# A hybrid decoder layer: both products of the rotary turn made by VectorE straight from PSUM

## Chip, cores, metric

One core of a Trainium2 chip. The metric is the device time of one execution in microseconds. The kernel before was timed three times; each comparison is against that kernel.

## What is computed

One layer with two groups of heads that run side by side, then a last RMSNorm. `x` is (1, 2048, 1024) in float32. The part that this document is about is the rotation of the attention heads' q and k by position:

```python
h = rmsnorm(x, norm_w) * (1.0 + scale) + shift
proj = h @ w_in                       # columns: deltanet q,k,v | z | b | a | at_q | at_k | at_v | at_z
o_dn = gated_delta_rule(...)          # 4 heads x 128: short convolution, chunked scan
aq, ak = rope(at_q, positions), rope(at_k, positions)   # 8 heads x 64
o_at = dilated_attention(aq, ak, av)
x = x + gate * (concat(o_dn * silu(z), o_at * silu(at_z)) @ w_out)
return rmsnorm(x)

def rope(x, positions):               # half = 32
    x1, x2 = x[..., :half], x[..., half:]
    return concatenate([x1 * cos - x2 * sin, x2 * cos + x1 * sin], axis=-1)
```

## The kernel before

Matrices are multiplied as three products of high and low halves (`three`, L612), so a 128x512 piece of the projection takes 24 matmuls, 8 blocks of depth by 3. The sequence is worked through in two halves of 1024 positions, each in two pieces `jj` of J = 512. The input projection is cut into 16 units of 256 columns; a unit is loaded, split into high and low halves (ScalarE casts `w_hi` at L580, POOL subtracts to `w_lo` at L581) and multiplied into PSUM tiles of the tag `ip`, of which there are two banks (`proj`, L622). Eight units are the deltanet heads' (`dn_unit`, L951: projection, convolution `cv_y`, then the solve `dn_intra` and `dn_solve` with `tmp_inv` and `rs_u`, and a scan `dn_scan` whose steps go between TensorE, VectorE and ScalarE by way of `y`, `state` and `o`). Units 8 to 11 are q and k of the attention heads and go through `rope_unit` (L1016). `ORDER` sets which units fill the time between two deltanet heads; each of the units 8 to 11 is done in both halves, so there are 16 pieces `jj` with two column tiles `ct` each: 32 rotations.

In `rope_unit` the columns are laid out so that `ct` 0 holds the first halves x1 of four heads and `ct` 1 their second halves x2. For each piece two tables (cosine and sine, 128x512) are loaded from DRAM (L1025). For each `ct` the projection ends in a PSUM bank; ScalarE copies the bank to SBUF (`rx`, L1031) and VectorE multiplies the bank by the cosine table (L1033; the trace calls all products `rp`). When both are there, POOL multiplies the copy of the other `ct` by the sine table (L1041, `rp` too), VectorE subtracts or adds (`rpc`, L1045), and a generator in the queue `late` splits the result (ScalarE `r_hi` L1052, POOL `r_lo` L1053) and writes it to DRAM (L1055), from where the attention reads it after the last rotation. The SBUF tiles of 128x512 come from one ring of nine buffers, tag `t512`, that the convolution, the gates and others share.

The program is written as generators that are stepped in turn (`tick`, L200): after each step of the main one, the solves, the scans and the rest each add a few instructions. The framework then lays out each engine's stream in a list by priority and by the times at which it estimates that instructions are ready; `Early` marks the scan's instructions as more urgent. An engine runs its stream in that order.

Of the kernel before, what the change touches and what calls it, by code (L numbers as in the profile page):

```python
# [11 lines left out]
F32 = mybir.dt.float32  # L12
# [3 lines left out]
OP = mybir.AluOpType  # L16
# [5 lines left out]
P = 128  # L22
KT = D // P
J = 512
# [6 lines left out]
T5 = 9  # L31
# [81 lines left out]
def kernel(ctx: ExitStack, tc: tile.TileContext, x, c_t, pos, w_mod, b_mod_t, b_gate,  # L113
# [3 lines left out]
    V, A, G = nc.vector, nc.scalar, nc.gpsimd  # L117
# [482 lines left out]
    def load_unit(u):  # L600
        w = w_tiles()
        if saved[u]:
            for a in range(2):
                dma(columns(u, w, a), wscr[u][a])
            return w
        for _ in unit_parts(u, w):
            pass
        saved[u] = True
        late.append(keep(u, w, KEEP))
        return w  # L610
# [11 lines left out]
    def proj(w, h, ct):  # L622

        ps = bank("ip")
        yield from three(ps, [lambda k, p=p: w[p][:, k, ct * P:ct * P + P] for p in range(2)],
                         [lambda k, p=p: h[p][:, k, :] for p in range(2)], KT)
        return ps
# [388 lines left out]
    def rope_unit(fa, u, js, hs, w):  # L1016
        w = w or load_unit(u)
        scr = (qscr, kscr)[u >= 10][u % 2]
        for jj in range(2):
            if jj:  # L1020
                yield "part"
            tab = [fa.tile([P, J], F32, name="tab", tag="t512", bufs=T5) for _ in range(2)]
            for i in range(2):
                c = ctab[i, js[jj]]
                dma(tab[i], bass.AP(tensor=c.tensor, offset=c.offset, ap=[[J, 32], [0, 4], [1, J]]))  # L1025
            xs, p1s = [], []
            for ct in range(2):
                ps = yield from proj(w, hs[jj], ct)
                by_class = ps.rearrange("p (i r) -> p r i", r=4)
                t = fa.tile([P, J], F32, name="rx", tag="t512", bufs=T5)  # L1030
                A.copy(t.rearrange("p (r i) -> p r i", r=4), by_class)  # L1031
                p1 = fa.tile([P, J], F32, name="rp1", tag="t512", bufs=T5)
                V.tensor_tensor(p1.rearrange("p (r i) -> p r i", r=4), by_class,  # L1033
                                tab[0].rearrange("p (r i) -> p r i", r=4), OP.mult)
                xs.append(t)
                p1s.append(p1)
                yield
            for ct in range(2):
                p1 = p1s[ct]
                p2 = fa.tile([P, J], F32, name="rp2", tag="t512", bufs=T5)  # L1040
                G.tensor_tensor(p2, xs[1 - ct], tab[1], OP.mult)  # L1041
                hi = fa.tile([P, J], F32R, name="r_hi", tag="r32", bufs=R3)
                lo = fa.tile([P, J], F32R, name="r_lo", tag="r32", bufs=R3)
                pc = fa.tile([P, J], F32, name="rpc", tag="t512", bufs=T5)
                V.tensor_tensor(pc, p1, p2, (OP.subtract, OP.add)[ct])  # L1045
                late.append(split(pc, hi, lo, scr, ct, js[jj]))
                if RY:
                    yield

    def split(pc, hi, lo, scr, ct, j):  # L1050
        yield from hop(RL)
        A.copy(hi, pc)  # L1052
        G.tensor_tensor(lo, pc, hi, OP.subtract)  # L1053
        for i, a in enumerate((hi, lo)):
            dma(scr[i, :, 32 * ct:32 * ct + 32, j].rearrange("h c t -> c h t"), a.bitcast(F32))  # L1055
# [5 lines left out]
    fa = fa_ctx.__enter__()  # L1061
# [346 lines left out]
    with (tc.tile_pool(name="start", bufs=1, side="left", reuse_waits="tile") as sp,  # L1408
          tc.tile_pool(name="fx0", bufs=2, side="left", reuse_waits="tile") as fx0):
        ordered[0] = OD  # L1410
        tab = tables(sp)
        h0, w12, wk, acc, xs = start(fa, sp, fx0)
# [337 lines left out]
```

## Time and profile before

| | us |
|---|---|
| median of three runs | 1560.82 (1558.38 to 1561.52) |
| profiled execution | 1564.69 |
| its span | 1562.9 |
| TensorE busy | 1433.8 |
| VectorE busy | 1066.2 |
| ScalarE busy | 656.0 |
| POOL busy | 466.1 |

The profile is one execution. Engines are named PE (TensorE; PEld is its loading of weights), DVE (VectorE), ACT (ScalarE), POOL and SP (which issues DMAs). An instruction is named by its line and by its tiles, out<-in. L138 stands for all that is recorded by the wrapper for urgent instructions, L149 for all matmuls. The idle time ahead of an instruction is put down to what ended last of what it waited for. A hole in PE is found in the timeline as the number in brackets.

### The profile page before, as it was taken

To read this page: it belongs to the slowest core of one execution; us is meant where nothing else is said; L and a number is where in the kernel's file an instruction comes from. 1 tells how busy PE (TensorE), PEld (TensorE's weight loads), DVE (VectorE), ACT (ScalarE), POOL (GpSimd) and SP (SyncE) were. 2 spreads that over 40 slices of the span, in tenths; PEclk is the share of its full clock that TensorE was granted. 3 is DMA by queue.
4 is the path that set the end of the run, shared out by engine and by line. 5 is a ranking of instruction groups with operands and counts; after the bars stand their busy time and mean duration, and the time that the engine had idled before them with its cause. 6 is when DMAs were issued, how large, how long until landed. Compare 5 with 4: busy or idle time off the path is not lost.

```text
span 1562.9 us, 28358 instructions
## 1 busy us (share of the span) xinstructions
PE 1433.8 (92%) x9848; PEld 1156.7 (74%) x9848; DVE 1066.2 (68%) x3305; ACT 656.0 (42%) x1864; POOL 466.1 (30%) x573
## 2 busy tenths in 40 slices
PE   3898999989879999998999999998899998999997
PEld 2687787767767787876777779886677776777776
DVE  6868745684786367587687766434476776889766
ACT  4435234335433753433243343222455554576444
POOL 2424253333452432041231320223121211142243
PEclk9999999999999999999999999999999999999999
DMA  8845562546573642454434515438877637363364
GB/s 245 277 135 192 162 206 81 176 133 212 178 225 97 226 132 87 155 177 129 152 99 129 159 39 154 148 106 259 248 224 212 205 108 229 89 197 104 105 226 162
DMA packets 256336, 257.08 MB, mean 164 GB/s; under 512 B 44993, under 2 KB 196673, under 8 KB 255681
## 3 DMA queue, kind: packets, MB, share of 16 engines
q1 hardware_dynamic: 253744, 246.88, 51.1%
q10 hardware_dynamic: 2448, 8.39, 1.4%
q8 instruction: 78, 1.28, 0.3%
q14 instruction: 66, 0.53, 0.1%
HBM read 164.31 MB, written 90.90 MB: 163 GB/s over the span
## 4 chain that ended last, share of the span: by engine, by line
PE 36%; DVE 10%; DMA 4%; ACT 2%; issue 2%; POOL 1%; SPq 1%; DVEq 0%; ACTq 0%; POOLq 0%
PE ip L149 16%; PE s L149 8%; PE tr L154 5%; PE po L149 4%; PE g L149 2%; PE sc L149 2%; DVE cv_y L693 1%; DMA sscr<-sta 1%; DMA wg<-in_w_mod_dram 1%; DVE tmp_inv L807 1%; DVE rs_u L282 1%; DVE pts L1251 1%; DMA y_lo<-in_w_out_dram 1%; DVE sm L1226 1%; DVE rs_u L281 0%
## 5 line engine op out<-in xcount | busy, mean ns | idle before, releaser
L149 PE MATMUL ip<-h_hi,w_hi 128*128 128x512 f32 x864 | 352.8, 410 | 6.0 <-ACT cv_r L688 4.7
L149 PE MATMUL ip<-h_hi,w_lo 128*128 128x512 f32 x864 | 352.6, 410 | 0.0
L149 PE MATMUL ip<-h_lo,w_hi 128*128 128x512 f32 x864 | 352.5, 410 | 0.0
L149 PEld LDWEIGHTS ip<-h_hi,w_hi 128*128 128x128 f32 x864 | 165.9, 192 | 39.3 <-ACT cv_r L688 5.6
L149 PEld LDWEIGHTS ip<-h_lo,w_hi 128*128 128x128 f32 x864 | 165.3, 191 | 32.2 <-issue 0.5
L149 PEld LDWEIGHTS ip<-h_hi,w_lo 128*128 128x128 f32 x864 | 165.1, 191 | 32.2 <-issue 0.8
L693 DVE SCALAR_TENSOR_TENSOR cv_y<-cv_r,cw,cv_y 128x512 f32<-128x512 f32 x144 | 116.0, 805 | 32.9 <-ACT cv_y L690 23.0
L581 POOL TENSOR_TENSOR w_lo<-w_raw,w_hi 128x512 fp32r<-128x512 f32 x72 | 97.0, 1357 | 112.4 <-ACT w_hi L580 84.7
L1226 DVE CUSTOM_DVE_ANT_0 sm<-s,mask 128x256 f32<-128x256 f32 (+3 forms) x256 | 107.9, 447 | 21.4 <-PE s L149 10.7
L154 PE MATMUL tr<-cst,p 128*128 128x128 f32 x568 | 95.3, 289 | 4.2 <-ACT p L1229 2.7
L1251 DVE COPY pts<-tr 128x512 f32<-128x512 f32 (+1 forms) x120 | 73.1, 616 | 30.7 <-PE tr L154 29.2
L1229 ACT ACTIVATE p<-sm,stb 128x128 f32<-128x128 f32 (+3 forms) x128 | 70.9, 555 | 52.4 <-DVE stb L1226 39.9
L1229 ACT ACTIVATE p<-sm,sta 128x256 f32<-128x256 f32 (+1 forms) x128 | 63.2, 495 | 68.7 <-DVE sta L1226 61.9
L154 PEld LDWEIGHTS tr<-cst,p 128*128 128x128 f32 x568 | 62.1, 142 | 25.4 <-issue 14.6
L695 ACT ACTIVATE cv_t<-cv_y 128x512 f32<-128x512 f32 x48 | 30.3, 631 | 117.6 <-DVE cv_y L693 114.1
L149 PE MATMUL ip<-w_hi,h_hi 128*128 128x264 f32 (+1 forms) x256 | 75.4, 295 | 2.0 <-DVE rp L1033 1.3
L149 PE MATMUL ip<-w_hi,h_lo 128*128 128x264 f32 (+1 forms) x256 | 75.0, 293 | 0.0
L149 PE MATMUL ip<-w_lo,h_hi 128*128 128x264 f32 (+1 forms) x256 | 74.9, 293 | 0.0
L807 DVE TENSOR_TENSOR tmp_inv<-xt_inv,blk 128x8 f32<-128x8 f32 (+14 forms) x240 | 65.6, 273 | 6.4
L580 ACT CAST w_hi<-w_raw 128x512 fp32r<-128x512 f32 x72 | 43.6, 617 | 49.4 <-DMA w_raw<-in_w_in_dram 40.9
L138 ACT ACTIVATE sqo<-o 128x128 f32<-128x128 f32 x64 | 19.8, 309 | 103.0 <-DVE o L138 97.3
L1041 POOL TENSOR_TENSOR rp<-rx,tab 128x512 f32<-128x512 f32 x32 | 41.5, 1312 | 57.5 <-ACT rx L1031 48.5
(470 smaller groups left out, 3372.9 us busy)
## 6 DMA issues: line engine op xcount, KB each, us to landing
w_raw<-in_w_in_dram SPq DMA_DIRECT2D x72, 256.0 KB, 3.9
ws<-w_hi SPq DMA_DIRECT2D x15, 1024.0 KB, 5.5
ws<-w_lo SPq DMA_DIRECT2D x15, 1024.0 KB, 7.4
w_hi<-ws SPq DMA_DIRECT2D x15, 1024.0 KB, 6.0
w_lo<-ws SPq DMA_DIRECT2D x15, 1024.0 KB, 7.5
xt<-in_x_dram SPq DMA_DIRECT2D x24, 512.0 KB, 5.2
wm<-in_w_mod_dram SPq DMA_DIRECT2D x32, 256.0 KB, 5.4
tab<-ctab SPq DMA_DIRECT2D x32, 256.0 KB, 3.3
```

Of the source, the lines that this page charges most:

```text
L138: return f(*a, **k)
L149: i = self.engine.matmul(ps, lhsT=lhsT, rhs=rhs, **k)
L154: i = self.engine.transpose(*a)
L580: A.copy(hi[:, s, 0:256], raw)
L581: G.tensor_tensor(lo[:, s, 0:256], raw, hi[:, s, 0:256], OP.subtract)
L693: V.scalar_tensor_tensor(y, r[:, n:n + J], cw[:, ti, n:n + 1], y, op0=OP.mult, op1=OP.add)
L695: A.activation(t, y, AF.Tanh)
L807: V.tensor_tensor(tmp[:, :, 0:i + 1], xt[:, :, 0:i + 1], b3[:, i:i + 1, 0:i + 1].to_broadcast([P, 4, i + 1]), OP.mult)
L1041: G.tensor_tensor(p2, xs[1 - ct], tab[1], OP.mult)
L1226: V.tensor_tensor_reduce(out=sm, in0=pp[hd], in1=masks, scale=-0.125, scalar=BIG, op0=OP.add, op1=OP.min, accum_out=st[:, slot, hd:hd + 1])
L1229: A.activation(pt, sm, AF.Exp, scale=-1.0, bias=st[:, slot, hd:hd + 1], accum_out=st[:, slot, 2 + hd:3 + hd])
L1251: V.tensor_copy(pts[:, 0:kn], pt[:, 0:kn])
```

## The change

ScalarE's copy and POOL's sine product are gone. In the loop over `ct`, VectorE multiplies the PSUM bank by the cosine table and then by the sine table, both in the transposed view `by_class`; the second loop only picks the two products that belong together. The rest of the rotation is the same.

```diff
-            xs, p1s = [], []
+            turned_ = []
             for ct in range(2):
                 ps = yield from proj(w, hs[jj], ct)
                 by_class = ps.rearrange("p (i r) -> p r i", r=4)
-                t = fa.tile([P, J], F32, name="rx", tag="t512", bufs=T5)
-                A.copy(t.rearrange("p (r i) -> p r i", r=4), by_class)
-                p1 = fa.tile([P, J], F32, name="rp1", tag="t512", bufs=T5)
-                V.tensor_tensor(p1.rearrange("p (r i) -> p r i", r=4), by_class,
-                                tab[0].rearrange("p (r i) -> p r i", r=4), OP.mult)
-                xs.append(t)
-                p1s.append(p1)
+                two = []
+                for i in range(2):
+                    t = fa.tile([P, J], F32, name=("rc", "rs")[i], tag="t512", bufs=T5)
+                    V.tensor_tensor(t.rearrange("p (r i) -> p r i", r=4), by_class,
+                                    tab[i].rearrange("p (r i) -> p r i", r=4), OP.mult)
+                    two.append(t)
+                turned_.append(two)
                 yield
             for ct in range(2):
-                p1 = p1s[ct]
-                p2 = fa.tile([P, J], F32, name="rp2", tag="t512", bufs=T5)
-                G.tensor_tensor(p2, xs[1 - ct], tab[1], OP.mult)
+                p1, p2 = turned_[ct][0], turned_[1 - ct][1]
```

## Rows read from the trace of the kernel before

**Rows 1.** The page, part 1: busy us (share of span) xinstructions.
```profile
PE 1433.8 (92%) x9848; PEld 1156.7 (74%) x9848; DVE 1066.2 (68%) x3305; ACT 656.0 (42%) x1864; POOL 466.1 (30%) x573
```
**Rows 2.** Busy time in the stretch of all rotations: length, busy per engine, clock, DMA.
```profile
150.00:1045.00 895.00, 845.36 (x5927) 683.94 (x5926) 589.73 (x1809) 331.97 (x968) 280.49 (x396) 0.98 0.47 148
```
**Rows 3.** Waits of PE from 150 to 1045 us: total us, times, longest.
```profile
PE sc L149 <- DVE state L138: 11.9, 12, 3.2
PE g L149 <- DVE qk L776: 10.0, 3, 6.6
...
PE ip L149 <- DVE rp L1033: 2.5, 3, 1.3
```
**Rows 4.** Groups by line and form, whole span: busy us, mean ns | idle before.
```profile
L1041 POOL TENSOR_TENSOR rp<-rx,tab 128x512 f32<-128x512 f32 x32 | 41.5, 1312 | 57.5 <-ACT rx L1031 48.5 <-issue 8.2 <-DMA oscr<-oc 0.5
...
L1045 DVE TENSOR_TENSOR rpc<-rp,rp 128x512 f32<-128x512 f32 x32 | 38.0, 1206 | 11.2 <-POOL rp L1041 11.2
...
L1033 DVE TENSOR_TENSOR rp<-ip,tab 128x512 f32<-128x512 f32 x32 | 22.0, 687 | 24.9 <-ACT rx L1031 24.8
...
L1031 ACT COPY rx<-ip 128x512 f32<-128x512 f32 x32 | 18.6, 581 | 30.4 <-PE ip L149 29.5 <-POOL xc L138 0.9
```
**Rows 5.** Instructions on the tile rp: ns min/median/max, first and last start.
```profile
L1033 DVE TENSOR_TENSOR rp<-ip,tab x32: 677/691/694, 169.0 to 1026.7; 128x512 f32<-128x512 f32 x32
...
L1045 DVE TENSOR_TENSOR rpc<-rp,rp x32: 678/926/1830, 179.3 to 1030.5; 128x512 f32<-128x512 f32 x32
```
**Rows 6.** Timeline of DVE near 430 us: start, length, instruction [idle before].
```profile
426.26 0.69 DVE L1033 TENSOR_TENSOR rp<-ip,tab 128x512 f32<-128x512 f32 x1
428.41 1.75 DVE L1045 TENSOR_TENSOR rpc<-rp,rp 128x512 f32<-128x512 f32 x1 [1.45 <-POOL rp L1041]
431.35 1.74 DVE L1045 TENSOR_TENSOR rpc<-rp,rp 128x512 f32<-128x512 f32 x1 [1.19 <-POOL rp L1041]
433.02 0.34 DVE L138 SCALAR_TENSOR_TENSOR y<-sc,sc,vs 128x128 f32<-128x128 f32 x1
...
433.42 0.17 DVE L807 TENSOR_TENSOR tmp_inv<-xt_inv,blk 128x8 f32<-128x8 f32 x1
```
**Rows 7.** Timelines of PE: the four holes that the sum names, and one matmul.
```profile
178.52 0.39 PE L149 MATMUL ip<-w_hi,h_hi 128*128 128x256 f32 x1 [1.26 <-DVE rp L1033]
...
402.55 0.47 PE L149 MATMUL ip<-h_hi,w_hi 128*128 128x512 f32 x1 [0.94 <-DVE rp L1033]
...
409.23 0.58 PE L149 MATMUL sc<-state,kq 128*128 128x128 f32 x1 [3.20 <-DVE state L138]
...
427.78 0.28 PE L149 MATMUL sc<-state,kq 128*128 128x128 f32 x1
...
434.07 0.38 PE L149 MATMUL sc<-y,inv 128*128 128x128 f32 x1 [2.29 <-ACT o L138]
```
**Rows 8.** Timeline of DVE near 405 us.
```profile
404.12 1.28 DVE L283 SCALAR_TENSOR_TENSOR xrs<-rs_u,xrs 128x8 f32<-128x8 f32 x1
405.44 1.20 DVE L281 TENSOR_TENSOR rs_u<-xrs 128x8 f32<-128x8 f32 x1
```
**Rows 9.** Timeline of POOL in the same stretch.
```profile
404.09 2.52 POOL L1041 TENSOR_TENSOR rp<-rx,tab 128x512 f32<-128x512 f32 x2
```
**Rows 10.** Busy time around two of the holes, columns as in Rows 2.
```profile
408.00:416.00 8.00, 6.77 (x23) 5.65 (x23) 7.29 (x23) 3.37 (x6) 3.67 (x3) 0.57 0.35 132
433.00:436.00 3.00, 1.93 (x9) 1.65 (x10) 2.73 (x11) 2.56 (x6) 1.40 (x2) 1.00 0.96 351
```
**Rows 11.** Timeline of DVE near 174 us.
```profile
173.72 0.98 DVE L807 TENSOR_TENSOR tmp_inv<-xt_inv,blk 128x8 f32<-128x8 f32 x1
...
174.94 1.01 DVE L807 TENSOR_TENSOR tmp_inv<-xt_inv,blk 128x12 f32<-128x12 f32 x1
```
**Rows 12.** Waits of SP's queue, whole span: the loads of the tables.
```profile
SPq L1025 <- POOL rp L1041: 11.7, 4, 8.6
```

## The prediction

> **What bounds the kernel now.** I read the page first: TensorE (PE) is busy 92% of the span, VectorE (DVE) 68% [rows 1]. So the time is TensorE's work plus the holes in it, and an edit on the other engines counts only where it opens, widens or closes a hole. Second, the stretch from 150 to 1045 us, where all 32 rotations lie (two pieces of 128x512 in each of 16 half stages; the cosine products start from 169.0 to 1026.7 us [rows 5]): TensorE is busy 845.36 of 895 us, so 49.6 us of holes are all that the change can act on directly [rows 2]. Third, what ends those holes: the rotation's own cosine product ends 2.5 us of them (it holds a projection's PSUM bank), the scan's state update on VectorE 11.9, the pair kk/qk on VectorE 10.0 [rows 3]. So VectorE's in-order queue is what TensorE waits for there, and the question is whether the change makes that queue shorter or longer at those places. Behind 1045 us no rotation runs, and the attention that reads the rotated q and k from DRAM starts later than that; a rotation that ends some us earlier or later moves nothing there.
>
> **What goes and what comes, engine by engine.** ScalarE loses 32 copies of 581 ns, 18.6 us; POOL loses 32 sine products of 1312 ns, 41.5 us [rows 4]. VectorE gets 32 sine products. They have the form of its cosine products (PSUM bank and one SBUF table in, SBUF out), which take 687 ns: 32 x 0.687 = +22.0 us [rows 4]. No DMA is added, moved or removed. Per half stage the ring of nine 128x512 buffers gives out 8 tiles in place of 10 (no copy, no separate sine tile: 2 tables, 4 products, 2 results), so a table's load on SP's queue, which four times waited for a POOL product to free a buffer, 11.7 us in all [rows 12], waits less; nothing behind it on SP's queue gets later. I count this at nothing, since TensorE's holes in [rows 3] are not ended by a DMA, and a gain is its only direction.
>
> **The port between VectorE and POOL.** The second thing VectorE loses is a stall. The combining subtraction or addition (two SBUF inputs) takes 678 ns at the least and 1830 at the most, the cosine product from PSUM 677 to 694 [rows 5]. The long ones lie beside a POOL product: in the two that start at 428.41 and 431.35 VectorE first idles 1.45 and 1.19 us for POOL's sine product, then needs 1.75 and 1.74 us [rows 6]; small instructions beside POOL's pair at 404.09 take 1.28 and 1.20 us where a small one elsewhere takes 0.17 [rows 6, 8, 9]. So a VectorE instruction with two SBUF inputs stands still until POOL's ends; one with a PSUM input does not. [...] With POOL's products gone the 32 combinations, 38.0 us at a mean of 1206 ns [rows 4], fall to somewhere between 690 ns (22 us in all) and no gain at all, since POOL still makes the low halves of weights and of the rotated tiles; I take 850 ns, nearer the free value because the partner that stood directly beside them is what goes: 38.0 - 27.2 = -10.8. The 11.2 us for which VectorE waited for POOL's product [rows 4] go whole. The cosine product waited 24.8 us for ScalarE's copy [rows 4], since both read one bank and the trace shows them one after the other; VectorE will now wait for TensorE's last matmul itself, so each such wait shrinks by up to one copy of 0.58. How many there are the row doesn't say, so between 0 and -18.6 (all 32); I count a fifth, -3.7, the value near no gain, since a busy VectorE comes to most of them late anyway. VectorE's time, busy and blocked together: +22.0 - 10.8 - 11.2 - 3.7 = -3.7 us, bounds +22.0 - 0 - 11.2 - 0 = +10.8 and 22.0 - 16 - 11.2 - 18.6 = -23.8. In total, then, VectorE's queue hardly changes; it is the places that decide.
>
> [...]
>
> **The holes, one by one** [rows 7].
> - At 434.07, 2.29 us: the scan's y (VectorE) started at 433.02 only because the two combinations ahead of it waited for POOL and were slowed by it [rows 6]. Without POOL's products they would follow the cosine product of 426.26 and the new sine product, 426.26 + 0.69 + 0.69 + 2 x 0.69, and end by 429 to 430; the matmul that y reads had begun at 427.78 [rows 6, 7]. The hole goes: -2.3.
> - At 409.23, 3.20 us, for the state update. Ahead of it on VectorE two small instructions lost 1.28 - 0.17 and 1.20 - 0.17 = 2.14 us to POOL's pair [rows 8, 9]; two sine products of 0.69 come in ahead of it. Net -0.76, the hole about 2.4. [...] Estimate from the row: 6.77 us busy x (1 - 0.57) = 2.9 us lost to the clock. A hole of 2.4 us is nearer to the 2.29 that kept the clock than to the 3.20 that lost it, so I count the 2.9 as saved, with 0 as the other bound: -3.7 together.
> - At 178.52, 1.26 us, for the bank: the cosine product stood behind two small instructions of 0.98 and 1.01 us beside POOL's pair, the first of them 0.17 elsewhere [rows 6, 11]: -1.65. The bank now comes free one product later: +0.69. Net -0.96.
> - At 402.55, 0.94 us, for the bank, where VectorE was merely late: +0.69.
> - Elsewhere a state update may stand behind an added product. Of the other 11 waits for it [rows 3] between none and all do; I take about half, five. There 0.69 comes and the stretch of a combination (1.206 - 0.69 = 0.5) goes: +0.2 each, +1.0.
> Sum: -2.3 - 3.7 - 1.0 + 0.7 + 1.0 = -5.3 us. The profiled execution took 1564.69 us (span 1562.9 and 1.8 around it), so 1559.4 by its own time; it ran 3.9 us above the median of 1560.82, and I give the forecast against that median: **1555.5 us**.
>
> **Rivals.**
> - *Hidden anyway.* Holes are closed and others open a little later, as TensorE meets the next late instruction; or the clock falls all the same behind 409. The sum without the clock is -2.4, and with nothing kept 0: 1558.5 to 1561. For it: the directly ended holes are 2.5 us only [rows 3]. Against: TensorE is 92% busy, so what it gains it mostly keeps.
> - *VectorE becomes late (slower).* Each added product delays what is queued behind it by 0.69 us, two per half stage. Where it lies ahead of a state update, a y or a kk/qk for which TensorE already stands, and no POOL stall is lifted in the same place, the hole widens by it. It decides from the point where more of TensorE's holes have such a product ahead of them than have a POOL stall. Price: eight such places (somewhat under half of the 18 waits counted in [rows 3]) x 0.69 = +5.5, 1566.3 us; if one of them grows past 3 us, the clock adds 2.9 as above. For it: those 18 waits are all VectorE's. Against: its busy and blocked time falls by my count.
> - *The planner lays the streams differently.* The order on each engine is set at the build from priorities and estimated ready times. With other costs on three engines it can put an instruction ahead of or behind a scan step anywhere behind 168 us, in the attention too. The price is one large hole more or less: the longest that ends with VectorE's qk is 6.6 us [rows 3], so 1554 or 1567, either sign.
> - *It doesn't do what it says:* the same products with the same tables, so no.
>
> **How the numbers follow.** About 0.2% (3.1 us) is what a measurement of this kernel can tell from no change. The forecast has 0.58, of which 0.44 lands beyond 0.2% and 0.14 inside (its clock part fails); hidden 0.12, all inside; VectorE late 0.16, slower; the planner 0.14: 0.06 faster, 0.02 the same, 0.06 slower. Faster 0.50, same 0.28, slower 0.22. The forecast's own range is 1550 (all holes named gone whole, 2.29 + 3.20 + 2.9 + 1.26 + 0.94 = 10.6) to 1560. The range is 1550 to 1567: its lower end is that one, its upper end takes in late VectorE and the bad side of the planner, and what is left out is several such mishaps at once.
>
> **What the profile after would show.** Right: sine and cosine products both at about 690 ns, 64 of them, 44 us; combinations near 850 ns with no wait for POOL; POOL about 41 and ScalarE about 19 us less busy; TensorE busy as before; no hole of 2.3 us behind a rotation, and the clock full where it fell at 409. Wrong: combinations still near 1200 ns (then other POOL work was the partner), holes on the state update or on the bank longer than 11.9 and 2.5 us in all, or large holes in places with no rotation near, which would be the planner's.

## Result and profile after

The changed kernel takes 1545.63 us in the median of six runs (1538.31 to 1550.44), the kernel before 1562.59 in six (1558.38 to 1563.82). The ratio is 0.9884, 95% interval 0.9863 to 0.9905: some 18 us less, where 5.3 were forecast and the range ended at 1550.

The profiled execution took 1541.81 us, its span is 1540.0. Against the span before, 1562.9, that is -22.9, more than the 18 of the ratio: 1541.81 lies low among the six of after, and the 1564.69 of the profiled execution before above its six. The page of after, part 1, in the columns of [rows 1]:

```profile
PE 1425.7 (93%) x9848; PEld 1153.4 (75%) x9848; DVE 1064.3 (69%) x3337; ACT 641.0 (42%) x1832; POOL 421.0 (27%) x541
```

TensorE does the same 9848 instructions. Its holes, span less busy time, went from 1562.9 - 1433.8 = 129.1 to 1540.0 - 1425.7 = 114.3, that is -14.8; the other -8.1 is busy time, the same work at a higher clock (granted share from 150 to 1045 us 0.98 [rows 2], in after 0.99). VectorE has 32 instructions more, 21.8 us of them, and is not busier: 1066.2 [rows 1] to 1064.3.

The groups of the rotation in after, columns as in [rows 4]:

```profile
L1051 POOL TENSOR_TENSOR r_lo<-rpc,r_hi 128x512 fp32r<-128x512 f32 x32 | 42.8, 1339 | 108.1 <-ACT r_hi L1050 43.8 <-issue 31.2 <-PE g L149 15.5
...
L1043 DVE TENSOR_TENSOR rpc<-rc,rs 128x512 f32<-128x512 f32 x32 | 26.5, 852 | 0.4
...
L1033 DVE TENSOR_TENSOR rc<-ip,tab 128x512 f32<-128x512 f32 x32 | 21.9, 685 | 15.6 <-PE ip L149 10.7 <-DMA tab<-ctab 3.4 <-POOL xc L138 1.4
L1033 DVE TENSOR_TENSOR rs<-ip,tab 128x512 f32<-128x512 f32 x32 | 21.8, 681 | 1.3 <-ACT xsq L529 1.2
```

The new sine product `rs` costs what the cosine product costs, the combination fell from 1206 [rows 4] to 852 ns, and its wait for POOL is gone. Those are the sizes that the forecast gave them.

TensorE's waits, first of after, then the rows of before that [rows 3] left out; both from 150 to 1000 us, where the holes of before sum to 49.6 us and those of after to 35.5 (neither has one from there to 1045):

```profile
PE sc L149 <- DVE state L138: 9.8, 9, 2.3
PE g L149 <- DVE qk L776: 8.3, 3, 5.3
PE g L149 <- DVE xt_inv L809: 4.9, 2, 2.8
PE g L149 <- issue: 3.7, 2, 2.7
...
PE g L149 <- ACT w L138: 1.9, 2, 1.5
PE ip L149 <- DVE rs L1033: 1.3, 1, 1.3
...
PE sc L149 <- ACT y L138: 0.3, 1, 0.3
```
```profile
PE g L149 <- issue: 9.0, 2, 4.8
PE sc L149 <- ACT o L138: 4.4, 4, 2.3
PE g L149 <- DVE xt_inv L809: 3.9, 3, 1.6
...
PE sc L149 <- ACT y L138: 2.2, 3, 1.1
```

The steps of the scan (`state`, `o`, `y`) ended 11.9 + 4.4 + 2.2 = 18.5 us of holes before and 9.8 + 0.3 = 10.1 after: there lies more than half of what the holes lost. The product that holds a projection's bank ended 2.5 us before and 1.3 after, but that isn't a gain: one of the three holes, 0.94 us at 402.55, is 1.09 in after and only stands under another name (`xrs`).

**Where along the way.** The order of TensorE's matmuls is nearly the same in both kernels, so they can be matched one to one. The lead of after (start before less start after) grows like this, steps under 0.45 us left out and neighbouring ones taken together:

| matmul, start before / after | lead | what it is |
|---|---|---|
| 178.52 / 177.67 | +1.4 | named in the forecast |
| 199.08 / 199.12 | -1.3 | new: the bank waits for the added sine product |
| 206.27 / 205.44, 276.90 / 276.41, 283.62 / 282.19 | +0.8, -1.0, +0.9 | a bank, a longer wait for `state`, one for `y` gone |
| 327.88 / 322.25, and the matmuls behind it | +3.2, +2.4 | hole put down to "issue", clock behind it |
| 335.52 / 329.05 to 368.76 / 365.92 | -5.2 | given back: two longer holes, a fall of the clock behind the second, small steps |
| 395.61 / 390.82 | +2.0 | mostly order: nine small matmuls that stood ahead of it come later in after; a hole of 0.30 is gone |
| to 402.55 / 398.72 | -1.0 | seven of the nine; the named hole, 0.94, is 1.09 |
| 409.23 / 402.38, and behind it | +3.0, +2.8 | named: hole, clock |
| 416.95 / 407.73 to 419.61 / 411.73 | -1.8 | the other two of the nine, new wait for `state` |
| 434.07 / 423.82 | +2.5 | named |
| 448.77 / 437.43 to 478.91 / 465.88 | +2.8 | +4.2 as at 328, of which 1.4 are given back |
| 478.91 / 465.88 to 828.70 / 806.77 | +8.9 | twelve steps of 0.5 to 1.8, two of them back; six in the scan |

The named places give 1.4 - 0.2 (the hole at 402.55 alone) + 5.8 + 2.5 = 9.5; the forecast had 6.3 for them. The other 13 us of the 22.9 came in places for which it had a loss of 1.0. One of them, before: VectorE, then POOL, then TensorE (start, length, instruction).

```profile
791.36 1.28 DVE L281 TENSOR_TENSOR rs_u<-sc 128x4 f32<-128x4 f32 x1
792.68 0.96 DVE L282 SCALAR_TENSOR_TENSOR rs_u<-rs_u,ss 128x4 f32<-128x4 f32 x1
793.68 0.96 DVE L283 SCALAR_TENSOR_TENSOR sc<-rs_u,sc 128x4 f32<-128x4 f32 x1
794.56 0.34 DVE L138 SCALAR_TENSOR_TENSOR y<-sc,sc,vs 128x128 f32<-128x128 f32 x1
```
```profile
791.35 1.28 POOL L1053 TENSOR_TENSOR r_lo<-rpc,r_hi 128x512 fp32r<-128x512 f32 x1
792.59 1.04 POOL L716 TENSOR_TENSOR gmghi<-cst,ghi 128x512 fp32r<-128x512 f32 x1
793.59 1.03 POOL L716 TENSOR_TENSOR gmglo<-cst,glo 128x512 fp32r<-128x512 f32 x1
```
```profile
795.36 0.49 PE L149 MATMUL sc<-y,inv 128*128 128x128 f32 x2 [1.74 <-ACT o L138]
```

Three small instructions of a solve, which take 0.16 to 0.17 us elsewhere, end each with one of POOL's. The scan's `y` stands behind them on VectorE, and TensorE waits for it. No rotation product is there; POOL's three are reads that after still makes. The same matmul in after starts at 774.01 without a hole; there VectorE's `y` came before POOL's next long read (VectorE, then POOL):

```profile
771.84 0.34 DVE L138 SCALAR_TENSOR_TENSOR y<-sc,sc,vs 128x128 f32<-128x128 f32 x1
```
```profile
772.72 1.74 POOL L1051 TENSOR_TENSOR r_lo<-rpc,r_hi 128x512 fp32r<-128x512 f32 x1 [0.90 <-DMA qscr<-r_hi]
```

### The profile page after: what moved, and what is told of

Same layout as the page of the kernel before. It is cut to its first block, busy times and chain, and to the rows that moved or that the text cites. A ratio compares the mean times of both kernels' runs of the same rounds, so it can differ in the third digit from the quotient of the medians.

```text
span 1540.0 us, 28271 instructions
## 1 busy us (share of the span) xinstructions
PE 1425.7 (93%) x9848; PEld 1153.4 (75%) x9848; DVE 1064.3 (69%) x3337; ACT 641.0 (42%) x1832; POOL 421.0 (27%) x541
## 3 DMA queue, kind: packets, MB, share of 16 engines
q8 instruction: 78, 1.28, 0.3%
## 4 chain that ended last, share of the span: by engine, by line
PE 44%; DVE 12%; DMA 7%; ACT 3%; issue 2%; POOL 1%; SPq 1%; DVEq 0%; ACTq 0%; POOLq 0%
PE ip L149 21%; PE s L149 8%; PE tr L154 6%; PE po L149 4%; PE g L149 3%; PE sc L149 3%; DVE cv_y L693 1%; DMA xt<-in_x_dram 1%; DVE tmp_inv L807 1%; DMA yscr<-m_x 1%; DMA wg<-in_w_mod_dram 1%; DMA sscr<-sta 1%; DVE rs_u L282 1%; ACT hf L557 1%; DVE rs_u L281 1%
## 5 line engine op out<-in xcount | busy, mean ns | idle before, releaser
L581 POOL TENSOR_TENSOR w_lo<-w_raw,w_hi 128x512 fp32r<-128x512 f32 x72 | 96.0, 1343 | 120.0 <-ACT w_hi L580 94.2
L1227 ACT ACTIVATE p<-sm,stb 128x128 f32<-128x128 f32 (+3 forms) x128 | 70.9, 555 | 49.6 <-DVE stb L1224 38.0
L1051 POOL TENSOR_TENSOR r_lo<-rpc,r_hi 128x512 fp32r<-128x512 f32 x32 | 42.8, 1339 | 108.1 <-ACT r_hi L1050 43.8
L807 DVE TENSOR_TENSOR tmp_inv<-xt_inv,blk 128x8 f32<-128x8 f32 (+14 forms) x240 | 61.1, 254 | 6.0
```

What stands on the lines that cost most here:

```text
L581: G.tensor_tensor(lo[:, s, 0:256], raw, hi[:, s, 0:256], OP.subtract)
L807: V.tensor_tensor(tmp[:, :, 0:i + 1], xt[:, :, 0:i + 1], b3[:, i:i + 1, 0:i + 1].to_broadcast([P, 4, i + 1]), OP.mult)
L1227: A.activation(pt, sm, AF.Exp, scale=-1.0, bias=st[:, slot, hd:hd + 1], accum_out=st[:, slot, 2 + hd:3 + hd])
```

## The experiments

Two theories. *The port:* while POOL reads SBUF with a sine product, VectorE's instructions with two SBUF inputs stand still, and that alone cost the 18 us. *The wait:* the combination waited for POOL's product and the cosine product for ScalarE's copy, and lifting these waits gave the gain. "Port" is a name only: no run shows by what way POOL's reading stops VectorE. Beside them stand the extra work on VectorE (rival "VectorE becomes late") and the order of the streams (rival "the planner").

**Both back, as work that nobody reads.** The changed kernel, with ScalarE's copy and POOL's product on top; the combination doesn't depend on them.

```diff
+                rx = fa.tile([P, J], F32, name="rx", tag="t512", bufs=T5)
+                A.copy(rx.rearrange("p (r i) -> p r i", r=4), by_class)
+                xs.append(rx)
...
+                idle = fa.tile([P, J], F32, name="rp2", tag="t512", bufs=T5)
+                G.tensor_tensor(idle, xs[1 - ct], tab[1], OP.mult)
```

> The changed kernel, with ScalarE's copy and POOL's sine product put back beside it: they run at their old place and cost, but nothing reads POOL's product, so it is work on top that leaves the output as it is. Theory of the wait (what was gained is that VectorE's queue no longer stands at the combination until ScalarE and POOL have passed the half on): the gain stays for the most part, 10 to 17 us under the kernel before, combinations wait for POOL 0 us. Theory of the port (what was gained is that POOL's 41.5 us no longer block VectorE's two-SBUF-input instructions): the gain goes, 0 to +5 us against the kernel before, since VectorE also does 22 us more; combinations back to 1.1 to 1.2 us. Theory of the planner: any value, with no relation to holes behind rotations.

Measured: 1565.16 against 1565.13, ratio 1.0004 (0.9981 to 1.0026). The whole gain is gone although no result of POOL's is used. The groups:

```profile
L1044 POOL TENSOR_TENSOR rp<-rx,tab 128x512 f32<-128x512 f32 x32 | 46.1, 1441 | 59.6 <-ACT rx L1031 19.5 <-DVE rc L1036 12.8 <-issue 12.7
...
L1048 DVE TENSOR_TENSOR rpc<-rc,rs 128x512 f32<-128x512 f32 x32 | 31.1, 985 | 6.8 <-POOL rp L1044 4.3 <-issue 2.1
```

The combination is slower than in after (985 against 852 ns), though not back at the 1.1 to 1.2 us expected. It still waits 4.3 us for POOL, where the kernel before has 11.2 [rows 4]; as it uses no result of POOL's, this can only be for a buffer of the ring. So the wait for the result is not the cause, and what is left of the wait is too short for 18 us; in the run with POOL copies below, 8.5 us of it go with a time 12 us shorter. It may still be POOL's reading, its time, or the copy.

**Only the copy back.** The first three added lines of the diff above.

> The changed kernel with ScalarE's copy put back, read by nobody. Theories of the wait and of the port alike: within 3 us of the changed kernel, 14 to 20 us under the kernel before, as the copy only holds the PSUM bank along with VectorE's first product. If the 18.6 us of ScalarE are the cause: the gain goes, 0 to -5.

Measured: 1547.17, ratio 0.9902 (0.9876 to 0.9928). The gain stays within the interval of after; the copy, and the cosine product's wait for it (19.4 us, against 24.8 [rows 4]), cost some 3 us by the two ratios, which can't be told from zero.

**VectorE's work alone.** The kernel before, with 32 sine products on VectorE that nobody reads.

```diff
+                idle = fa.tile([P, J], F32, name="rs", tag="t512", bufs=T5)
+                V.tensor_tensor(idle.rearrange("p (r i) -> p r i", r=4), by_class,
+                                tab[1].rearrange("p (r i) -> p r i", r=4), OP.mult)
```

> The kernel before with the 32 sine products on VectorE from PSUM on top, read by nobody; POOL and ScalarE do all they did. It measures the price of 22 us of VectorE alone, which the prediction put at 0.7 to 5.5 us: +1 to +6 us against the kernel before. If VectorE is where TensorE's holes come from, as much as +15; if its time is free there, 0 +- 2.

Measured: 1564.01, ratio 1.0006 (0.9986 to 1.0027): 22 us more on VectorE, from PSUM, cost nothing.

**POOL as long, but writing only.** As in the first experiment, the product replaced by three fills of about its length.

```diff
-                G.tensor_tensor(idle, xs[1 - ct], tab[1], OP.mult)
+                G.memset(xs[1 - ct], 0.0)
+                G.memset(idle, 0.0)
+                G.memset(idle[:, 0:192], 0.0)
```

> As the run with both put back, but in the place of POOL's sine product stand three fills with zeros (512, 512 and 192 columns), which wait for the same copy and together take about as long, 1.3 us; they write SBUF and read nothing. Work on top; the output stays. Port theory (POOL's product costs because it reads SBUF through what VectorE's second input needs): the time stays that of the copy alone put back, 12 to 17 us under the kernel before. Theory of POOL's queue (it costs because weights' low halves and the scan's small copies stand behind it on POOL): the gain is gone as in the run with both put back, 0 +- 3 us. In the trace, small VectorE instructions beside a fill are at 0.17 us under the port theory in either case; what decides is the time.

Measured: 1548.86 against 1566.08, ratio 0.9902 (0.9866 to 0.9937). The page's part 1, then the groups:

```profile
PE 1428.9 (92%) x9848; PEld 1154.7 (75%) x9848; DVE 1067.5 (69%) x3337; ACT 658.6 (43%) x1864; POOL 462.2 (30%) x637
```
```profile
L1045 POOL MEMSET rp<- 128x512 f32 x32 | 16.9, 527 | 3.2 <-DVE rs L1036 2.5 <-DVE rc L1036 0.7
L1044 POOL MEMSET rx<- 128x512 f32 x32 | 16.8, 526 | 74.3 <-ACT rx L1031 71.0 <-issue 3.3
...
L1046 POOL MEMSET rp<- 128x192 f32 x32 | 8.2, 259 | 1.6
```

POOL is as busy as before (462.2 against 466.1 [rows 1]), in the same place of its queue and behind the same copy, and the gain is there. Between this run and the first lie 1.0 point of ratio, some 16 us. TensorE's matmuls have the same order in both. They differ in whether POOL reads; besides, the product holds the sine table's buffer, which the fills don't, but TensorE's waits in the first run have a DMA in them for 0.3 us only. So it is the reading. It shows in single instructions too. The same small instruction with two SBUF inputs takes 1.24 us in the first run beside the product (VectorE, POOL) and 0.15 in this one beside a fill:

```profile
398.67 1.24 DVE L912 SCALAR_TENSOR_TENSOR so<-so,eq 128x4 f32<-128x4 f32 x1
```
```profile
398.60 1.29 POOL L1044 TENSOR_TENSOR rp<-rx,tab 128x512 f32<-128x512 f32 x1
```
```profile
395.54 0.15 DVE L912 SCALAR_TENSOR_TENSOR so<-so,eq 128x4 f32<-128x4 f32 x1
```
```profile
395.29 0.53 POOL L1045 MEMSET rp<- 128x512 f32 x1
```

**Short fills.** Two fills of 8 columns in the product's place: the waiting at the head of POOL's queue without the time.

> The same with two fills of 8 columns each: POOL only stands and waits for ScalarE's copy at that place, and works some 0.1 to 0.2 us. If the waiting at the head of POOL's queue is the cost: the gain is gone or half gone, 0 to -8 us against the kernel before. Under the port theory, and if it is POOL's time: 12 to 17 us under the kernel before, like the copy alone.

Measured: 1543.97, ratio 0.9862 (0.9831 to 0.9894), more under the kernel before (some 21 us) than the 12 to 17 expected, but not to be told from the long fills or from after.

**POOL reading one input.** The product replaced by two copies of the same tile.

```diff
-                G.tensor_tensor(idle, xs[1 - ct], tab[1], OP.mult)
+                G.tensor_copy(idle, xs[1 - ct])
+                G.tensor_copy(idle, xs[1 - ct])
```

> As the run with both put back, with two POOL copies of 512 columns (one SBUF input each, some 0.55 us) in the place of the sine product; work on top. It asks whether POOL must have two inputs to block VectorE. If any reading blocks: the gain goes by as much as the copies are long, to 0 to -6 us against the kernel before; if only two-input instructions block: 14 to 18 us under the kernel before, as with the fills.

Measured: 1553.43 against 1564.54, ratio 0.9930 (0.9908 to 0.9951).

```profile
L1049 DVE TENSOR_TENSOR rpc<-rc,rs 128x512 f32<-128x512 f32 x32 | 28.4, 899 | 8.8 <-POOL rp L1045 7.0 <-POOL rp L1044 1.5
L1044 POOL COPY rp<-rx 128x512 f32<-128x512 f32 x32 | 24.2, 756 | 60.5 <-ACT rx L1031 19.7 <-DVE rs L1036 13.3 <-DVE rc L1036 11.6
...
L1045 POOL COPY rp<-rx 128x512 f32<-128x512 f32 x32 | 23.7, 739 | 1.8
```

Against the copy alone (0.9902), 47.9 us of one-input reading cost some 4 us, which the intervals don't tell from nothing; against after (0.9884) some 7. The 46.1 us of two-input reading cost 16 and 19. So one-input reading costs less than two-input reading, between the two forecasts. Whether that is because each block is half as long (739 to 756 against 1441 ns) or because POOL reads one operand in place of two isn't settled.

**The sine product on VectorE, from the copy.** The kernel before, with L1041 moved from POOL to VectorE and nothing else (`G.tensor_tensor` becomes `V.tensor_tensor`).

> The kernel before with one letter changed: VectorE in place of POOL makes the sine product from ScalarE's copy in SBUF; the copy stays. TensorE's order is nearly that of the kernel before. Theory of the wait: POOL's part of the passing-on is gone and ScalarE's is left, so a half to all of the gain: -8 to -17 us. Theory of the port: POOL's products are gone, so the whole gain, -15 to -19, less up to 3 because the new products themselves have two SBUF inputs and can stand still beside POOL (mean over 0.8 us in place of 0.69). If ScalarE's copies are the cause: 0 to -3 us.

Measured: 1552.17, ratio 0.9922 (0.9893 to 0.9951). Two thirds of the gain come from that alone:

```profile
L1045 DVE TENSOR_TENSOR rpc<-rp,rp 128x512 f32<-128x512 f32 x32 | 29.7, 930 | 0.6
L1041 DVE TENSOR_TENSOR rp<-rx,tab 128x512 f32<-128x512 f32 x32 | 23.7, 742 | 0.5 <-issue 0.5
```

From SBUF the product has two SBUF inputs and takes 742 ns in the mean, with POOL's other reads still there (`r_lo` 44.9 us, `w_lo` 97.1); from PSUM, in after, it takes 681. Two operations follow the matmul here, and copying its output to SBUF ahead of the second brought nothing: 0.9922 with the copy, 0.9884 without.

**The two products in the other order.** The changed kernel with sine before cosine: the same work, a handful of instructions elsewhere in the streams.

```diff
-                for i in range(2):
+                for i in (1, 0):
```

> The changed kernel with the two products of a bank in the other order, sine ahead of cosine: the same work and waits, but the planner lays some instructions in other places. It measures what such a shift alone does: theory of the planner, 5 us or more either way from the changed kernel; otherwise within 3 us of it, 15 to 20 under the kernel before.

Measured: 1540.22 against 1564.54, ratio 0.9842 (0.9825 to 0.9858), some 6 us better than after (2 to 11 by the two intervals). A shift of order without any work in it is thus worth some 6 us; so much of any difference here, the 18 us too, can be order. The whole isn't: the five kernels without POOL's product or a reading in its place (after, the copy alone, both fills, this one) lie 15 to 25 us under the kernel before, and the two that keep the product (both back, VectorE's work alone) within 1 us of it.

**More of POOL's reading taken away.** If reading is the price, POOL's other two-input work has one too. The changed kernel with the subtraction `r_lo` (32), with every second `w_lo` (36 of 72), with both, and with `r_lo` and all `w_lo` on VectorE:

```diff
-        G.tensor_tensor(lo, pc, hi, OP.subtract)
+        V.tensor_tensor(lo, pc, hi, OP.subtract)
```

> The changed kernel, and the rotated tiles' low halves (32 subtractions with two SBUF inputs) also on VectorE in place of POOL. POOL loses 42.8 us of reading, VectorE gains some 27 us. Port theory: POOL's other readings cost as its products did, so faster than the changed kernel, 5 to 15 us, 22 to 30 under the kernel before. Theory that only the rotation's own wait mattered: no gain, 0 to +5 against the changed kernel.

Measured: 1535.15 against 1566.08, ratio 0.9810 (0.9768 to 0.9852).

```diff
-            G.tensor_tensor(lo[:, s, 0:256], raw, hi[:, s, 0:256], OP.subtract)
+            (G, V)[g % 2].tensor_tensor(lo[:, s, 0:256], raw, hi[:, s, 0:256], OP.subtract)
```

> The changed kernel, and every other low half of the weights (36 of 72) on VectorE in place of POOL: POOL loses 48 us of reading, VectorE gains 30 us. Port theory: faster than the changed kernel by 3 to 10 us. If VectorE is full by now: slower by up to 10.

Measured: 1540.00, ratio 0.9833 (0.9807 to 0.9858).

> Both moves that made the changed kernel faster, together: the rotated tiles' low halves and half of the weights' on VectorE. Port theory with time left on VectorE: 32 to 40 us under the kernel before. If VectorE has become the bound by then (60 us of subtractions more than in the changed kernel): no better than the first move alone, 26 to 31 under.

Measured: 1522.02 against 1564.54, ratio 0.9729 (0.9706 to 0.9752).

```diff
-            G.tensor_tensor(lo[:, s, 0:256], raw, hi[:, s, 0:256], OP.subtract)
+            V.tensor_tensor(lo[:, s, 0:256], raw, hi[:, s, 0:256], OP.subtract)
...
-        G.tensor_tensor(lo, pc, hi, OP.subtract)
+        V.tensor_tensor(lo, pc, hi, OP.subtract)
```

> The same with all of the weights' low halves on VectorE: POOL loses some 140 us of reading against the changed kernel, VectorE gains some 85. Port theory alone: 38 to 50 us under the kernel before. VectorE as the bound: slower than the run with half of them.

Measured: 1499.06, ratio 0.9579 (0.9549 to 0.9609), the best of all: 66 us less than before, 47 less than after. Its page, part 1, some groups, and the stretch from 150 to 1000 us:

```profile
PE 1416.2 (95%) x9848; PEld 1149.0 (77%) x9848; DVE 1057.4 (71%) x3441; ACT 643.4 (43%) x1832; POOL 292.8 (20%) x437
```
```profile
L581 DVE TENSOR_TENSOR w_lo<-w_raw,w_hi 128x512 fp32r<-128x512 f32 x72 | 49.4, 695 | 31.5 <-ACT w_hi L580 31.1
...
L1051 DVE TENSOR_TENSOR r_lo<-rpc,r_hi 128x512 fp32r<-128x512 f32 x32 | 22.6, 705 | 3.0 <-DMA qscr<-r_hi 1.7 <-DMA kscr<-r_hi 0.6 <-ACT o L138 0.5
...
L1043 DVE TENSOR_TENSOR rpc<-rc,rs 128x512 f32<-128x512 f32 x32 | 21.3, 683 | 2.3 <-issue 2.2
```
```profile
150.00:1000.00 850.00, 832.11 (x5939) 679.76 (x5938) 583.54 (x1894) 314.38 (x914) 137.43 (x282) 1.00 0.48 155
```

VectorE takes on 49.4 + 22.6 = 72.0 us and its busy time falls from 1064.3 to 1057.4: 79 us of its other instructions' busy time had been standing still. The combination is at its free value, 683 ns. TensorE's holes in the stretch are 850 - 832.11 = 17.9 us, against 35.5 in after in the same stretch of time, and the clock is 1.00. Taking both away gains more than either, and all of it most; the first two runs can't be told apart by their intervals. The last gained more than the 38 to 50 us that the port theory gave it, and the four don't separate the port from a second effect: VectorE makes a `w_lo` in 695 ns where POOL took 1343, so weights may be ready earlier.

## Why the prediction was wrong

The sign was right, the size was not: -5.3 forecast, -18 measured, below the range. Step by step:

- *What goes and what comes.* VectorE +22.0: measured +21.8. POOL -41.5 and ScalarE -18.6: POOL's busy time fell by 45.1, ScalarE's by 15.0. Right.
- *The port.* Combinations 850 ns, measured 852, which is luck in part: 850 was a choice between 690 and 1206, and the kernels without the product show 798 to 865. The wait for POOL's product -11.2, measured -10.8 (11.2 to 0.4). Right. The cosine product's waits -3.7: its idle time went from 24.9 to 15.6, and the sine product has 1.3, so -8.0. Too small, but the copy's run shows that this is worth little.
- *"VectorE's queue hardly changes."* This is the first wrong sentence. The ledger took up stalls of the combinations alone. Busy time: +21.8 for the sine products and 26.5 - 38.0 = -11.5 for the combinations make +10.2 with the cosine products' -0.1; measured 1064.3 - 1066.2 = -1.9. So 12.1 us were saved in other VectorE instructions that stood beside POOL's products. With the waits it is -1.9 - 10.8 - 8.0 = -20.7 against the forecast's -3.7, next to its lower bound of -23.8.
- *The holes, one by one.* 434.07: -2.5 for -2.3, right. 178.52: -1.4 for -0.96, right there, but 20 us on the bank waits 1.27 us for an added product, and the gain is gone. 409.23: -3.0 for -0.76, and the clock -2.8 for -2.9; the hole was mis-sized. 402.55: from 0.94 to 1.09, +0.15 for +0.69, and by another route: in after VectorE first stands 1.55 us for the load of a table, which the forecast counted at nothing. Of these, in after (PE, then VectorE):

```profile
199.12 0.36 PE L149 MATMUL ip<-w_hi,h_hi 128*128 128x256 f32 x1 [1.27 <-DVE rs L1033]
...
398.72 0.47 PE L149 MATMUL ip<-h_hi,w_hi 128*128 128x512 f32 x1 [1.09 <-DVE xrs L533]
...
402.38 0.71 PE L149 MATMUL sc<-state,kq 128*128 128x128 f32 x4 [0.20 <-DVE state L138]
...
411.73 0.71 PE L149 MATMUL sc<-state,kq 128*128 128x128 f32 x4 [1.14 <-DVE state L138]
```
```profile
397.20 0.69 DVE L1033 TENSOR_TENSOR rc<-ip,tab 128x512 f32<-128x512 f32 x1 [1.55 <-DMA tab<-ctab]
```

  The 3.20 us hole is 0.20. Ahead of `state` the two stalls beside POOL's pair [rows 8, 9] are gone, as forecast, and the combination that stood there before has moved behind it. A wait of 1.14 us for the next `state` is new.
- *"Elsewhere ... +1.0".* This is the step that failed. It looked at the holes that have a rotation product directly ahead of them, took five more waits for `state` at +0.2 each and every other place at nothing. In these places the lead grew by 13 us in the profiled pair. That POOL's reading is the cause of the sum is shown by the runs with products and with fills. How it reaches a single place was only followed in the example at 795 us: remaining reads of POOL's (`r_lo`, `gmghi`, `gmglo`) fall beside a solve before and behind it in after. That taking the products out of POOL's queue is what shifted them there is argued, not shown. Such a hole is put down to `state`, `o`, `y` or "issue", and as the example shows it needs no rotation near it.
- *The clock.* The forecast took one drop, at 409, and worked out its 2.9 us from the first row of [rows 10]. That a hole of 2.4 us would keep the clock was its estimate, which no run shows: in after this hole is 0.20 us, and the clock from 401 to 409 is 1.00. There were others: 0.62 and 0.66 before in stretches of which the matched ones in after have 1.00 and 0.83 (columns as in [rows 2], first two of before, then two of after):

```profile
325.00:334.00 9.00, 6.12 (x46) 4.92 (x47) 8.66 (x20) 1.93 (x4) 0.77 (x3) 0.62 0.43 126
462.00:472.00 10.00, 6.29 (x50) 5.07 (x51) 9.62 (x22) 1.83 (x3) 1.77 (x4) 0.66 0.51 159
```
```profile
320.00:329.00 9.00, 6.48 (x58) 4.67 (x56) 8.68 (x19) 2.62 (x6) 0.97 (x4) 1.00 0.40 115
448.00:458.00 10.00, 7.33 (x56) 5.59 (x55) 9.68 (x19) 1.83 (x3) 3.08 (x6) 0.83 0.68 216
```

  And one is new: in after the clock falls behind a hole of 2.81 us at 336.21. Before, this hole was 1.57 us and the clock stayed at 1.00 from 340 to 350. In after:

```profile
338.00:340.00 2.00, 2.00 (x6) 1.54 (x6) 1.85 (x7) 0.60 (x1) 0.12 (x1) 0.50 0.00 0
```

  In all, TensorE's busy time fell by 8.1 us, where 2.9 were forecast.
- *Hidden anyway.* True of two places: the 1.4 us won at 178.52 were given back at 199, and the 5.6 won around 328 us, but for 0.4, by 369 us. Elsewhere the lead stayed.
- *VectorE becomes late.* Priced at +5.5. The hole at 199.12 is such a place; but with 22 us put on VectorE alone, 1.0006 (0.9986 to 1.0027). The rows of [rows 3] are waits for VectorE, but in the sum not for its work: for its standing still.
- *The planner.* TensorE's stream is almost the same: of its 9848 instructions about ten changed their place. VectorE's is less so: at 409 the combination now stands behind `state`. A shift of a few gave 6 us in the run with the products swapped, so the sign is settled and the share of the order in the 18 is open by about that much.
- *The range.* Its low end, 1550, took all named holes as gone whole. The bound for the port's cost belonged there as well: 23.8 us on VectorE was written down as a bound of the ledger, and not carried into the range.

Open: how the 13 us divide among the places (the profiled pair is one execution each), the share of the order, and why one-input reading costs less.

## What to carry over

Before an elementwise operation with two SBUF inputs goes to POOL to relieve VectorE, count its duration as time in which VectorE's two-input instructions, the smallest ones above all (1.28 us in place of 0.16 at 791 us), can stand still: here POOL's reading cost 0.2 to 0.4 us of kernel time per us (18 for 41.5 us of products, 12 for 42.8 us of `r_lo`, 8 for half of 96.0 us of `w_lo`, 47 for all 138.8; each open by the 6 us of the order, and the last three hold also that VectorE does the work in a little over half the time, 695 to 775 ns where POOL took 1339 and 1343), while 22 us more on VectorE cost nothing. A busy share includes standing still (of VectorE's 1064.3 us in after 79 went with POOL's reading, in the last run), so an engine at 68% may have less to do than it shows. And where one engine stops another, don't sum only the holes that stand beside the edit: carry the bound of the whole stall into the range.

## What the runs showed of the hardware

- POOL's fills (write only, 527 ns for 128x512) didn't stop VectorE's two-input instructions: the combination takes 798 ns with them and 804 with the copy alone. Its two-input products (1441 ns) did, 985; its one-input copies (739 to 756 ns) less, 899.
- Not only two-input instructions stopped. In after, a one-input instruction on VectorE lies beside POOL's `r_lo` and takes 1.25 us, where the same one in the kernel before takes 0.17 (VectorE in after, POOL in after, VectorE before):

```profile
398.68 1.25 DVE L279 TENSOR_SCALAR xrs<-xrs 128x8 int32<-128x8 int32 x1
```
```profile
398.61 1.28 POOL L1051 TENSOR_TENSOR r_lo<-rpc,r_hi 128x512 fp32r<-128x512 f32 x1 [1.85 <-DMA qscr<-r_hi]
```
```profile
401.63 0.17 DVE L279 TENSOR_SCALAR xrs<-xrs 128x8 int32<-128x8 int32 x1
```

  The forecast took two-input instructions alone.
- VectorE made a 128x512 subtraction of two SBUF tiles in 695 to 705 ns (the last run), POOL in 1339 to 1343 (after), so moving it to VectorE about halved the time of the operation as well.
- Holes of 3.20 and 4.22 us are followed by stretches with a mean clock of 0.57 [rows 10] and 0.62, and one of 2.81 us in after by 0.50 from 338 to 340 us; one of 2.29 us by none [rows 10]. The length alone doesn't tell: before, a hole of 1.63 us at 478.91 is followed by 0.57 from 480 to 484. Closing the holes at 409 and 328 gave back nearly as much again in the clock as in the hole (3.0 and 2.8 us at 409, 3.2 and 2.4 at 328, where it was lost again behind the next long hole).
